# A first mixer's output projection with eight products instead of seven, and three moved steps

## The chip, the cores and the metric

The kernel runs on one core of a Trainium2 chip. The metric is the time of one execution on the device in microseconds (us), as the median of several runs. PE is TensorE (matmuls), PEld its weight loads, DVE VectorE, ACT ScalarE, POOL GpSimd, and SP the engine whose queue issues most of the DMAs.

## The reference, cut to what matters

A trunk of two layers on 512 tokens of width 1024. Each layer is a mixer, a cross-attention into 256 memory rows (4 heads of 256), and a gated MLP with a width-3 convolution; each sub-layer ends in `x = layer_norm(alpha * x + f(x))`. The first layer's mixer, which most of the change touches:

```python
proj = x @ w_in                                   # 1024 -> 1536
uv = gelu(proj[..., :1024]); u, v = uv[..., :512], uv[..., 512:]
v = layer_norm(v, ln_g, ln_b)
sp = einsum('gij,bnjgc->bnigc', masked(w_s), v in blocks of 128) + b_s
y_a = u * sp                                      # "gates", 4 groups of 128 channels
xb = proj[..., 1024:]                             # 4 groups, trailing means of 2, 4, 8, 16 tokens
pooled = trailing_mean(xb, window) - xb
y_b = einsum('bsgc,gcd->bsgd', pooled, pool_w) * pool_scale
return concatenate([y_a, y_b]) @ w_out            # 1024 -> 1024
```

The second layer's mixer is `w_out(B * conv3(C * h))` with `B, C, h` from one projection. All is float32.

## The kernel before, in words

**Precision.** Every operand of a matmul is split in two parts: `split` casts it on ACT to a high part (L86) and subtracts that on DVE for a low part (L87). `mm3` (L226 to L228) adds three matmuls, high x high, high x low and low x high. So each weight tile of 128 x 1024 costs one ACT cast and one DVE subtraction, and so does each activation.

**Weights.** `plan` lists all weight tiles in the order of use. `Weights.load` fetches up to three ahead by DMA into one of 7 `raw` tiles and splits the next into one of RING = 5 buffer pairs (`wh`, `wl`); each `weights.done()` sets off one such load when a tile has been used.

**Plain and fast products.** A plain output projection (`residual_norm`, L513 to L544) works by halves of 512 output columns. The first half runs over the 8 blocks of k, with the 4 token blocks t inside, into 4 PSUM banks, and then adds each bank to `xt[t]` (L491). The second half holds all four weight tiles, does one token block at a time, adds it, takes statistics (L499) and normalises it (`norm`, L336 to L341); at k = 2 of token blocks 2 and 3 it transposes blocks 0 and 1 of the new x (`to_feat`, L366). The transposes of blocks 2 and 3 are returned as a hook for the next stage.

A fast product (`fast_product`) does 7 block products in place of 8, in the manner of Strassen and Winograd. It needs sums of blocks on both sides: for the activations `Blocks` keeps two neighbouring feature blocks of y in a scratch tile and makes S1 to S4 of them on DVE (L277), then splits three or four blocks at a time (`act<-blocks`); for the weights POOL makes the sums t1 to t4 (L162, L169 to L171) from the raw tiles. It adds 16 banks to x (L382) where the plain form adds 8. `norm(3)` and both pairs of transposes are returned as hooks. Fast forms serve the first mixer's `ab_w_out`, the second's `c_w_out`, and the MLP's down projections but for the last group of layer 1.

**The first mixer** (`mixer_ab`): the v projection over tokens, its layer norm, four feature blocks of `ab_w_f` with the trailing means, then four feature blocks for u, each with its gelu (L615); pool blocks (`pool_block`) and gate blocks (`gate_block`) are woven in between them, and the y blocks go into `Blocks`. `FIRST` turns the order of the weights by two, since the pool halves come first.

**What follows.** `proj_k` makes the keys of layer 0's attention with 256-column matmuls, 24 to a weight tile; the hooks run ahead of its heads 1, 2 and 3. In layer 1, `proj_v` does, after the mixer's product. `attend` then does queries, scores with the softmax (DVE maximum, ACT exponential), `turn(h)` (transposes of head h's softmax) and `values(h)`.

**The order on each engine** is laid at build time by a planner, which takes the instructions that its own model holds ready, earlier ones in the program first; the hardware then runs each engine's list in that order. PSUM has 8 banks, all from one pool; activations share 12 slots.

Of the kernel before, what the change touches and what calls it, by code (L numbers as in the profile page):

```python
# [8 lines left out]
F32 = mybir.dt.float32  # L9
# [21 lines left out]
AHEAD = 3  # L31
FFN_GROUPS = (((0, 8), (8, 14), (14, 22)), ((0, 8), (8, 16), (16, 22)))
PAD = 16
FIRST = {"ab_w_out": 2}


@with_exitstack
def kernel(ctx: ExitStack, tc: tile.TileContext, a: dict, out: bass.AP):
# [73 lines left out]
    plan = []  # L112
    for layer in range(2):
        if layer == 0:
            plan += [("ab_w_v", i) for i in range(4)] + [("ab_w_f", i) for i in range(4)] + [("pool_w",)]
            plan += [("ab_w_f", i) for i in range(4, 8)]
            plan += fast_plan("ab_w_out", 0, 0, 4)
            plan += [("xa_wk", layer, i) for i in range(8)]
        else:
            plan += [("xa_wk", layer, i) for i in range(8)]  # L120
            plan += [("c_w_in", i) for i in range(24)]
            plan += fast_plan("c_w_out", 0, 0, 4)
        wq = [("xa_wq", layer, i) for i in range(8)]
        wv = [("xa_wv", layer, n, i) for n in range(2) for i in range(4)]
        plan += wv + wq if layer else wq + wv
        plan += [("xa_wo", layer, n, i) for n in range(2) for i in range(4)]
        for m0, m1 in FFN_GROUPS[layer]:
            plan += [("ffn_w_up", layer, i) for i in range(2 * m0, 2 * m1)]
            if layer == 0 or m1 < NF:
                plan += fast_plan("ffn_w_down", layer, m0 // 2, m1 // 2)  # L130
            else:
                plan += [("ffn_w_down", layer, n, i) for n in range(2) for i in range(m0 // 2, m1 // 2)]

    class Weights:
# [7 lines left out]
        def fast(self, what, name, layer, i, i0=None, i1=None):  # L142

            w = a[name][layer]
            half = [slice(0, 512), slice(512, CH)]

            def fetch(src):
                t = raw_tile()
                nc.sync.dma_start(t[:, : src.shape[-1]], src)
                return t  # L150

            def both(key, make=raw_tile):
                if key not in self.kept:
                    self.kept[key] = make()
                    self.sides[key] = 0
                self.sides[key] += 1
                return self.kept[key][:, half[self.sides[key] - 1]]

            at = (i + FIRST.get(name, 0)) % w.shape[1]
            if what == "b11b21":  # L160
                w0, w1 = fetch(w[0, at]), fetch(w[1, at][:, half[0]])
                nc.gpsimd.tensor_sub(both("t1"), w1[:, half[0]], w0[:, half[0]])  # L162
                return w0
            if what == "t2b22":
                w1, w0 = fetch(w[1, at]), fetch(w[0, at])
                self.turn += i == i0
                t3 = both(("t3", i0), lambda: row_tile("gb"[self.turn % 2]))
                b12 = t2 = w1[:, half[0]]
                nc.gpsimd.tensor_sub(t3, w1[:, half[1]], b12)  # L169
                nc.gpsimd.tensor_add(t2, t3, w0[:, half[0]])  # L170
                nc.gpsimd.tensor_sub(both(("t4", i0)), w0[:, half[1]], t2)  # L171
                return w1
            t = self.kept.pop({"t1t1": "t1", "t4t4": ("t4", i), "t3t3": ("t3", i)}[what])
            return t[:, : 512 * (i0 - i)]
# [372 lines left out]


    def mixer_ab(xT):
        vs, pads = slot(F32), slot(F32)  # L550
        v = [vs[:, t * 512 : (t + 1) * 512] for t in range(NT)]
        ps = [ps_tile() for _ in range(NT)]
        for k in range(KD):
            if k % 2 == 0:
                w = weights.take("ab_w_v", k // 2)
            for t in range(NT):
                proj_tok(ps[t], xT, k, t, w, k % 2, k == 0, k == KD - 1)
            if k % 2:
                weights.done()
        g, b = load_rows("sgu_ln_g", 0, AW, nc.sync), load_rows("sgu_ln_b", 0, AW, nc.sync)  # L560
        for t in range(NT):
            nc.scalar.activation(v[t], ps[t], AF.Gelu_apprx_tanh)
            st = spool.tile([P, 1, 6], F32, tag="stats1", name=nm("st"))
            nc.vector.bn_stats(st[:, 0, :], v[t])
            normalise(v[t], st, g, b)

        pooled = Act(4)
        for gi, win in enumerate(WINDOWS):
            (ps,) = proj_batch([("ab_w_f", gi)], xT)
            cur, *free = [pads[:, j * (PAD + S) : (j + 1) * (PAD + S)] for j in range(3)]  # L570
            xb = cur
            nc.gpsimd.memset(cur[:, :PAD], 0.0)
            nc.scalar.copy(cur[:, PAD:], ps)
            sh, lo = 1, 0
            while sh < win:
                nxt = free[0]
                lo += sh
                nc.vector.tensor_add(nxt[:, lo:], cur[:, lo:], cur[:, lo - sh : PAD + S - sh])
                free = [cur if cur is not xb else free[1]]
                cur, sh = nxt, sh * 2  # L580
            pl = tmp()
            e = win - 1
            nc.vector.scalar_tensor_tensor(pl, cur[:, PAD:], 1.0 / win, xb[:, PAD:], op0=ALU.mult, op1=ALU.subtract)
            nc.vector.tensor_mul(pl[:, :e], cur[:, PAD : PAD + e], inv[:, :e])
            nc.vector.tensor_sub(pl[:, :e], pl[:, :e], xb[:, PAD : PAD + e])
            split(pooled.h(gi), pooled.l(gi), pl)


        wsT, bsb = load_consts()
        y, pw = Blocks(), weights.take("pool_w")  # L590

        def pool_block(gi):
            ps = ps_tile()
            c = slice(gi * P, (gi + 1) * P)
            mm3(ps, pw[0][:, c], pw[1][:, c], pooled.h(gi), pooled.l(gi), True, True)
            y.put(gi, lambda to: nc.scalar.activation(to, ps.rearrange("p (i s) -> p i s", i=2), AF.Copy, scale=pscale[:, gi : gi + 1]))

        def gate_block(gi, ut):
            ps = ps_tile()
            for t in range(NT):  # L600
                nc.tensor.matmul(ps[:, t * P : (t + 1) * P], v[t][:, gi * P : (gi + 1) * P], wsT[:, gi, :], start=True, stop=True)
            sp = tmp()
            nc.vector.tensor_tensor(
                sp.rearrange("p (n i) -> p n i", n=NT),
                ps.rearrange("p (n i) -> p n i", n=NT),
                bsb[:, gi : gi + 1, :].to_broadcast([P, NT, P]),
                op=ALU.add,
            )
            y.put(gi, lambda to: nc.vector.tensor_mul(to, *(t.rearrange("p (i s) -> p i s", i=2) for t in (sp, ut))))

        last = None
        for gi in range(4):
            (ps,) = proj_batch([("ab_w_f", 4 + gi)], xT)
            ut = tmp()
            nc.scalar.activation(ut, ps, AF.Gelu_apprx_tanh)  # L615
            if gi < 2:
                pool_block(2 * gi)
                pool_block(2 * gi + 1)
            if gi == 1:
                weights.done()  # L620
            if last:
                gate_block(*last)
            last = gi, ut
        gate_block(*last)
        return y

    def conv3(dst, src, tap, bias=None):
# [62 lines left out]
    def attend(layer, xT, kT, v):  # L690
# [55 lines left out]
        if v is None:  # L746
            for m in range(8):
                queries(m, m + 1)
            o, v, mem = Act(8), {}, load_mem()
            scores(0)  # L750
            v[0] = proj_v(layer, mem, 0)
            turn(0)
            scores(1)
            values(0)
            v[1] = proj_v(layer, mem, 1)
            turn(1)
            scores(2)
            values(1)
        else:
            for m in range(6):  # L760
                queries(m, m + 1)
            scores(0)
            queries(6, 7)
            scores(1)
            queries(7, 8)
            o = Act(8)
            turn(0)
            scores(2)
            values(0)
            turn(1)  # L770
            values(1)

        def second():
# [45 lines left out]
    for layer in range(2):  # L819
        if layer == 0:  # L820
            y = mixer_ab(xT)
            xT, left = residual_norm([(lambda: y, 0, 8)], "ab_w_out", "ln_mix", layer, ahead=load_ahead)
            kT = proj_k(layer, mem.pop(), dict(zip((1, 2, 3), left)))
            v = None
        else:
            kT = proj_k(layer, mem.pop(), dict(zip((1, 2, 3), left)))
            y = mixer_c(xT)
            xT, left = residual_norm([(lambda: y, 0, 8)], "c_w_out", "ln_mix", layer, ahead=load_ahead)
            v = {0: proj_v(layer, mem[0], 0, {4: left[0]}), 1: proj_v(layer, mem.pop(), 1, {0: left[1], 6: left[2]})}
        o, hooks = attend(layer, xT, kT, v)  # L830
        xT, left = residual_norm([(lambda: o, 0, 8)], "xa_wo", "ln_xa", layer, hooks=hooks)
        up = [(lambda m0=m0, m1=m1, xT=xT, late=left[0]: ffn_up(layer, xT, late, m0, m1), m0, m1) for m0, m1 in FFN_GROUPS[layer]]
# [76 lines left out]
```

## Time and profile before

| | us |
|---|---|
| median of 3 runs | 1351.86 |
| lowest, highest | 1350.41, 1353.79 |
| the profiled execution | 1348.82 |
| its span, first to last instruction | 1347.1 |

| engine | busy us | share of the span |
|---|---|---|
| PE | 1320.3 | 98% |
| PEld (beside PE) | 1108.6 | 82% |
| DVE | 912.7 | 68% |
| ACT | 519.8 | 39% |
| POOL | 220.5 | 16% |

The share is a mean over stages with different limits. PE's idle time is put down, in the profile, to the instruction that ended it: `<-DVE x L382` is a wait until DVE had done line 382. The granted clock is PE's, 1.00 being full speed; matmuls are pipelined, so the time from one start to the next is what one costs, not the duration in its row. A name such as `ps<-act,wh` reads: bank from moving operand, stationary operand.

### The profile page before, as it was taken

How to read it: one execution, taken by the hardware profiler on the slowest of the kernel's cores; microseconds unless marked ns; L12 is line 12 of the kernel's file. 1: busy time of each engine (PE TensorE's matmuls, PEld its weight loads, DVE VectorE, ACT ScalarE, POOL GpSimd, SP SyncE). 2: the span in 40 equal slices, each digit the busy share in tenths (PEclk: the TensorE clock that was granted, in tenths of full speed). 3: DMA queues.
4: the chain of work that ended last, by engine and by line, in shares of the span. 5: the costliest groups of instructions: out<-in, count | busy, mean ns of one | idle time of the engine just before them, and what ended most of it. 6: DMA issues, size and time to landing. Idle time of an engine off the chain costs nothing. (4 is left out here: it accounts for less than half of the span.)

```text
span 1347.1 us, 16309 instructions
## 1 busy us (share of the span) xinstructions
PE 1320.3 (98%) x6373; PEld 1108.6 (82%) x6373; DVE 912.7 (68%) x1165; ACT 519.8 (39%) x665; POOL 220.5 (16%) x176
## 2 busy tenths in 40 slices
PE   9988999999999999999999999999999999999997
PEld 7867988889888888887988887788898888888885
DVE  6898746586676676669945569846676685577446
ACT  6444435324443443434423334434144343343330
POOL 1251100010240220033100142100000330141001
PEclk9989999999999999999999999999999999999999
DMA  8536634122345244236433237531133353236301
GB/s 315 164 111 203 203 109 149 54 80 86 102 146 159 82 138 156 86 118 224 157 110 104 81 108 249 189 94 47 47 94 102 111 179 118 86 115 229 94 0 63
DMA packets 50621, 170.51 MB, mean 127 GB/s; under 512 B 6000, under 2 KB 6128, under 8 KB 50544
## 3 DMA queue, kind: packets, MB, share of 16 engines
q1 hardware_dynamic: 48816, 163.18, 37.3%
q0 software_dynamic: 1728, 6.29, 1.5%
q8 instruction: 50, 0.82, 0.2%
q14 instruction: 27, 0.22, 0.0%
HBM read 167.35 MB, written 2.10 MB: 126 GB/s over the span
## 5 line engine op out<-in xcount | busy, mean ns | idle before, releaser
L87 DVE TENSOR_TENSOR wl<-raw,wh 128x1024 fp32r<-128x1024 f32 (+1 forms) x279 | 351.0, 1265 | 241.4 <-ACT wh L86 238.2
L86 ACT CAST wh<-raw 128x1024 fp32r<-128x1024 f32 (+1 forms) x279 | 290.7, 1042 | 518.1 <-PE ps L227 283.3
L226 PE MATMUL ps<-act,wh 128*128 128x512 f32 (+1 forms) x1284 | 472.5, 369 | 1.2 <-DVE act L87 1.1
L227 PE MATMUL ps<-act,wh 128*128 128x512 f32 (+1 forms) x1284 | 472.5, 368 | 0.1
L228 PE MATMUL ps<-act,wl 128*128 128x512 f32 (+1 forms) x1284 | 472.4, 368 | 0.0
L226 PEld LDWEIGHTS ps<-act,wh 128*128 128x128 f32 x1284 | 241.9, 189 | 42.2 <-DVE act L87 2.3
L227 PEld LDWEIGHTS ps<-act,wh 128*128 128x128 f32 x1284 | 242.1, 189 | 40.4 <-DVE act L87 0.4
L228 PEld LDWEIGHTS ps<-act,wl 128*128 128x128 f32 x1284 | 242.0, 189 | 40.1
L226 PE MATMUL ps<-wh,act 128*128 128x512 f32 (+1 forms) x656 | 257.1, 393 | 8.4 <-ACT tmp L615 4.6
L227 PE MATMUL ps<-wl,act 128*128 128x512 f32 (+1 forms) x656 | 256.3, 391 | 3.0 <-DVE wl L87 3.0
L228 PE MATMUL ps<-wh,act 128*128 128x512 f32 (+1 forms) x656 | 255.5, 389 | 0.0
L226 PEld LDWEIGHTS ps<-wh,act 128*128 128x128 f32 x656 | 124.1, 189 | 37.4 <-DVE x L382 5.9
L227 PEld LDWEIGHTS ps<-wl,act 128*128 128x128 f32 x656 | 124.2, 189 | 30.3 <-DVE wl L87 5.8
L228 PEld LDWEIGHTS ps<-wh,act 128*128 128x128 f32 x656 | 123.9, 189 | 25.3
L338 POOL TENSOR_TENSOR rs<-rs,mhalf 128x1 f32<-128x1 f32 x28 | 39.7, 1418 | 484.0 <-DVE rs L337 484.0
L162 POOL TENSOR_TENSOR raw<-raw,raw 128x512 f32<-128x512 f32 x27 | 39.4, 1460 | 458.9 <-DVE wl L87 379.5
L87 DVE TENSOR_TENSOR act<-blocks,act 128x768 fp32r<-128x768 f32 (+1 forms) x54 | 75.5, 1410 | 9.7 <-ACT act L86 9.7
L86 ACT CAST act<-ps 128x512 fp32r<-128x512 f32 x104 | 56.1, 594 | 60.5 <-PE ps L366 39.3
L382 DVE SCALAR_TENSOR_TENSOR x<-x,ps 128x512 f32<-128x512 f32 x112 | 72.0, 680 | 10.8 <-PE ps L228 10.8
L87 DVE TENSOR_TENSOR act<-ps,act 128x512 fp32r<-128x512 f32 x104 | 67.2, 683 | 12.9 <-ACT act L86 12.9
L86 ACT CAST act<-blocks 128x768 fp32r<-128x768 f32 (+1 forms) x54 | 49.1, 942 | 64.6 <-DVE blocks L277 64.6
L793 DVE TENSOR_TENSOR blocks<-tmp,ps 128x512 f32<-128x512 f32 x38 | 26.1, 688 | 59.8 <-PE ps L228 58.4
(80 smaller groups left out, 859.2 us busy)
## 6 DMA issues: line engine op xcount, KB each, us to landing
raw<-in_ffn_w_up SPq DMA_DIRECT2D x88, 512.0 KB, 3.6
raw<-in_ffn_w_down SPq DMA_DIRECT2D x63, 512.0 KB, 3.6
raw<-in_c_w_in SPq DMA_DIRECT2D x24, 512.0 KB, 3.5
raw<-in_xa_wk SPq DMA_DIRECT2D x16, 512.0 KB, 4.8
raw<-in_xa_wq SPq DMA_DIRECT2D x16, 512.0 KB, 3.6
raw<-in_xa_wv SPq DMA_DIRECT2D x16, 512.0 KB, 4.7
raw<-in_xa_wo SPq DMA_DIRECT2D x16, 512.0 KB, 4.0
raw<-in_ab_w_out SPq DMA_DIRECT2D x12, 512.0 KB, 3.6
```

Of the source, the lines that this page charges most:

```text
L86: nc.scalar.copy(h, src)
L87: nc.vector.tensor_sub(l, src, h.bitcast(F32))
L162: nc.gpsimd.tensor_sub(both("t1"), w1[:, half[0]], w0[:, half[0]])
L226: nc.tensor.matmul(ps, lh, rh, start=start, stop=False, skip_group_check=more)
L227: nc.tensor.matmul(ps, lh, rl, start=False, stop=False, skip_group_check=more)
L228: nc.tensor.matmul(ps, ll, rh, start=False, stop=stop, skip_group_check=more)
L338: nc.gpsimd.tensor_tensor(rs, rs, mhalf, op=ALU.pow)
L382: return nc.vector.scalar_tensor_tensor(z, z, scale, ps, op0=ALU.mult, op1=ALU.add)
L793: hid.put(m, lambda to: nc.vector.tensor_mul(to, *(v.rearrange("p (i s) -> p i s", i=2) for v in (g, ps[2 * i + 1]))))
```

## The change

1. **The first mixer in the plain form.** The four u blocks come first, and their gelus go into a slot of their own; then four gate blocks, then four pool blocks, each split into an ordinary activation (`Act`). `pool_w` moves behind the u weights in the plan.
2. **Its output projection in the plain form:** eight weight tiles in place of fourteen, no block sums, norms and the transposes of token blocks 0 and 1 within the product. Only the transposes of blocks 2 and 3 remain as a hook, at `proj_k`'s head 2. The `FIRST` turn goes.
3. **Layer 1:** `norm(3)` behind the fast `c_w_out` moves from k = 4 to k = 2 of the first `proj_v`, and the transposes of blocks 2 and 3 from k = 6 to k = 5 of the second.
4. **Layer 1's attention:** `turn(1)` stands ahead of `values(0)`.

```diff
-            plan += [("ab_w_v", i) for i in range(4)] + [("ab_w_f", i) for i in range(4)] + [("pool_w",)]
-            plan += [("ab_w_f", i) for i in range(4, 8)]
-            plan += fast_plan("ab_w_out", 0, 0, 4)
+            plan += [("ab_w_v", i) for i in range(4)] + [("ab_w_f", i) for i in range(8)] + [("pool_w",)]
+            plan += [("ab_w_out", 0, n, i) for n in range(2) for i in range(4)]
...
-        vs, pads = slot(F32), slot(F32)
+        vs, us, pads = slot(F32), slot(F32), slot(F32)
...
         wsT, bsb = load_consts()
-        y, pw = Blocks(), weights.take("pool_w")
...
+        u = []
+        for gi in range(4):
+            (ps,) = proj_batch([("ab_w_f", 4 + gi)], xT)
+            ut = us[:, gi * 512 : (gi + 1) * 512]
+            nc.scalar.activation(ut, ps, AF.Gelu_apprx_tanh)
+            u.append(ut)
+
+        y = Act(8)
+        pw = weights.take("pool_w")
+        for gi in range(4):
             ps = ps_tile()
             for t in range(NT):
                 nc.tensor.matmul(ps[:, t * P : (t + 1) * P], v[t][:, gi * P : (gi + 1) * P], wsT[:, gi, :], start=True, stop=True)
...
-            y.put(gi, lambda to: nc.vector.tensor_mul(to, *(t.rearrange("p (i s) -> p i s", i=2) for t in (sp, ut))))
+            nc.vector.tensor_mul(sp, sp, u[gi])
+            split(y.h(gi), y.l(gi), sp)
         for gi in range(4):
+            ps = ps_tile()
+            c = slice(gi * P, (gi + 1) * P)
+            mm3(ps, pw[0][:, c], pw[1][:, c], pooled.h(gi), pooled.l(gi), True, True)
+            yb = tmp()
+            nc.scalar.activation(yb, ps, AF.Copy, scale=pscale[:, gi : gi + 1])
+            split(y.h(4 + gi), y.l(4 + gi), yb)
+        weights.done()
         return y
...
             o = Act(8)
             turn(0)
             scores(2)
+            turn(1)
             values(0)
-            turn(1)
             values(1)
...
-            kT = proj_k(layer, mem.pop(), dict(zip((1, 2, 3), left)))
+            kT = proj_k(layer, mem.pop(), {2: left[0]})
...
-            v = {0: proj_v(layer, mem[0], 0, {4: left[0]}), 1: proj_v(layer, mem.pop(), 1, {0: left[1], 6: left[2]})}
+            v = {0: proj_v(layer, mem[0], 0, {2: left[0]}), 1: proj_v(layer, mem.pop(), 1, {0: left[1], 5: left[2]})}
```

More of the change, by code (lines that the diff above doesn't have):

```diff
@@ L33 @@
 PAD = 16
-FIRST = {"ab_w_out": 2}
 @with_exitstack
@@ L157, in both @@
                 return self.kept[key][:, half[self.sides[key] - 1]]
-            at = (i + FIRST.get(name, 0)) % w.shape[1]
             if what == "b11b21":
-                w0, w1 = fetch(w[0, at]), fetch(w[1, at][:, half[0]])
+                w0, w1 = fetch(w[0, i]), fetch(w[1, i][:, half[0]])
                 nc.gpsimd.tensor_sub(both("t1"), w1[:, half[0]], w0[:, half[0]])
@@ L164, in fast @@
             if what == "t2b22":
-                w1, w0 = fetch(w[1, at]), fetch(w[0, at])
+                w1, w0 = fetch(w[1, i]), fetch(w[0, i])
                 self.turn += i == i0
@@ L589, in mixer_ab @@
         wsT, bsb = load_consts()
-        y, pw = Blocks(), weights.take("pool_w")
[L592 to L598, printed above, removed]
+        u = []
[7 more added lines that the diff above has]
+        for gi in range(4):
             ps = ps_tile()
@@ L608, in gate_block @@
             )
-            y.put(gi, lambda to: nc.vector.tensor_mul(to, *(t.rearrange("p (i s) -> p i s", i=2) for t in (sp, ut))))
-        last = None
+            nc.vector.tensor_mul(sp, sp, u[gi])
+            split(y.h(gi), y.l(gi), sp)
         for gi in range(4):
[L613 to L624, printed above, removed]
+            ps = ps_tile()
[5 more added lines that the diff above has]
+        weights.done()
         return y
```

## The prediction

> **What bounds the kernel now.** I read the page first (part 1), then busy time by windows, then TensorE (PE) in order of time, then the groups.
>
> ```profile
> PE 1320.3 (98%) x6373; PEld 1108.6 (82%) x6373; DVE 912.7 (68%) x1165; ACT 519.8 (39%) x665; POOL 220.5 (16%) x176
> ```
>
> PE is busy for 98% of the span, so a microsecond counts only if PE stands still or has more or fewer matmuls. The windows say where it stands still. Columns: stretch, length, busy time and instructions of PE, PEld, DVE, ACT, POOL, granted clock, DMA share, GB/s.
>
> ```profile
> 26.84:62.20 35.36, 35.36 (x157) 29.29 (x156) 31.84 (x54) 12.27 (x19) 10.88 (x12) 1.00 0.52 174
> 62.20:76.60 14.40, 14.40 (x82) 12.50 (x80) 12.61 (x15) 8.77 (x11) 6.28 (x5) 1.00 0.39 114
> 76.60:128.64 52.04, 43.32 (x171) 33.73 (x170) 47.73 (x56) 20.16 (x21) 18.62 (x12) 0.90 0.55 175
> 128.64:156.39 27.75, 27.00 (x225) 26.49 (x224) 27.75 (x39) 13.74 (x19) 4.95 (x5) 1.00 0.57 185
> ```
>
> The first row is projections without a pause: six feature blocks of 24 matmuls and four pool blocks of 3, 156 in 35.36 us, so one 512-column matmul costs **0.2267 us** of PE. The third row is the first output projection, from its first matmul to the first one of proj_k. Its seven half-products are 7 x 4 pairs x 2 halves x 3 = 168 matmuls, 38.08 us at that pace; it took 52.04. **13.96 us are lost there**. In order of time (start, duration, and in brackets the idle time with what ended it):
>
> ```profile
> 80.13 0.40 PE L228 MATMUL ps<-wh,act 128*128 128x512 f32 x1
> 85.16 0.80 PE L226 MATMUL ps<-wh,act 128*128 128x512 f32 x1 [4.63 <-ACT tmp L615]
> 89.55 0.40 PE L227 MATMUL ps<-wl,act 128*128 128x512 f32 x1
> ...
> 102.71 0.50 PE L226 MATMUL ps<-wh,act 128*128 128x512 f32 x1 [1.20 <-DVE x L382]
> ...
> 113.07 0.39 PE L226 MATMUL ps<-wh,act 128*128 128x512 f32 x1
> 115.40 0.50 PE L227 MATMUL ps<-wl,act 128*128 128x512 f32 x1 [1.95 <-DVE wl L87]
> 117.13 0.80 PE L226 MATMUL ps<-wh,act 128*128 128x512 f32 x1 [0.77 <-DVE x L382]
> 120.25 0.39 PE L227 MATMUL ps<-wl,act 128*128 128x512 f32 x1
> ```
>
> From 80.13 to 89.55 eleven matmuls start: 9.42 - 11 x 0.2267 = 6.93 us lost, of which 4.63 is the wait and 2.30 mostly the lower clock behind it. From 113.07 to 120.25, eleven again: 7.18 - 2.49 = 4.69 lost. Behind the 4.63 stands this on ACT:
>
> ```profile
> 81.89 1.78 ACT L86 CAST act<-blocks 128x768 fp32r<-128x768 f32 x2 [6.21 <-DVE blocks L277]
> 83.58 1.04 ACT L86 CAST wh<-raw 128x1024 fp32r<-128x1024 f32 x1
> 84.52 0.59 ACT L615 ACTIVATE tmp<-ps 128x512 f32<-128x512 f32 x1
> ```
>
> The last gelu (L615) had its bank full before the product began, but stood behind casts of block sums that DVE had not made; the product wanted that bank. All four waits of the stretch lead to DVE, which is busy 47.73 of 52.04 us. So here the chip is bound by DVE, not by PE.
>
> **The change part by part.** *The plain product.* It has 2 halves x 8 k x 4 t x 3 = 192 matmuls, 24 more: **+5.44 us** of PE, on the path. What it takes off DVE, by groups of 26.84 to 160 us (mean ns after the comma):
>
> ```profile
> L87 DVE TENSOR_TENSOR wl<-raw,wh 128x1024 fp32r<-128x1024 f32 (+1 forms) x30 | 41.1, 1384 | 4.5 <-ACT wh L86 4.4
> L87 DVE TENSOR_TENSOR act<-blocks,act 128x768 fp32r<-128x768 f32 (+1 forms) x8 | 10.8, 1372 | 2.1 <-ACT act L86 2.1
> L382 DVE SCALAR_TENSOR_TENSOR x<-x,ps 128x512 f32<-128x512 f32 x16 | 10.3, 677 | 0.0
> L277 DVE TENSOR_TENSOR blocks<-blocks 128x256 f32<-128x256 f32 x16 | 7.5, 481 | 0.3
> L609 DVE TENSOR_TENSOR blocks<-tmp,tmp 128x512 f32<-128x512 f32 x4 | 3.7, 954 | 0.0
> L87 DVE TENSOR_TENSOR act<-tmp,act 128x512 fp32r<-128x512 f32 x4 | 2.8, 690 | 2.1 <-ACT act L86 2.1
> ```
>
> Weight splits go from 14 to 8 (6 x 1.384 = 8.3 us), the 16 block sums go (7.5), eight block splits (10.8) become eight of 0.690 (5.5), and 16 adds to x become 8 (5.4 saved): 8.3 + 7.5 + 10.8 - 5.5 + 5.4 = 26.5 us less DVE work. That is nearly twice the 13.96 us lost, so I take the loss as gone: **-13.96 us**. The 16 weight sums on POOL and eight of the 16 weight loads in SP's queue go too; neither was on the path. The two row loads in POOL's queue move ahead of the product, into a queue with nothing else.
>
> Is the plain form free of waits? The kernel has it next door, the layer's xa_wo; second half and what follows it:
>
> ```profile
> 267.20:293.20 26.00, 26.00 (x124) 21.64 (x123) 21.97 (x32) 6.26 (x8) 4.37 (x3) 1.00 0.15 49
> 293.20:302.00 8.80, 8.80 (x76) 8.80 (x75) 7.52 (x10) 1.06 (x1) 1.46 (x1) 1.00 0.64 216
> ...
> 294.03 1.22 DVE L87 TENSOR_TENSOR wl<-raw,wh 128x1024 fp32r<-128x1024 f32 x1
> 295.77 1.21 DVE L87 TENSOR_TENSOR wl<-raw,wh 128x1024 fp32r<-128x1024 f32 x1
> 297.01 1.17 DVE L87 TENSOR_TENSOR wl<-raw,wh 128x1024 fp32r<-128x1024 f32 x1
> ```
>
> PE is busy throughout. The second half holds four of the five weight buffers to its end, so four loads must be split around the handover; three of these are ready 2.1, 3.8 and 5.0 us after 293.20. The follower there runs 256-column matmuls, 24 to a weight, as proj_k does, so it asks as fast as proj_k will. Adding load_mem's two splits (1.2 us each by the nearest wl rows) at the head of that half is hidden by the 4 us that DVE is idle in 26. Exit: 0.
>
> *The entry.* After: eight feature blocks from 26.84 end at 26.84 + 8 x 5.44 = 70.4; gates take 14.40 - 2 x 5.44 = 3.5, pools 2.7, so the product still starts at about 76.6. The first y: 71.2 + an add from a bank (0.677, as L382's) + L609's 0.954 + a cast (0.6, as L615's 0.59) + a split of 0.690 = 74.2, in time. Later gates follow DVE at 2.32 us each, and the k loop eats one in 12 x 0.2267 = 2.72. Banks bind more: eight are taken by gates and pools, and the fourth token block needs the fourth gate's add, at 71.2 + 3 x 2.32 + 0.68 = 78.9, where PE wants it at 76.6 + 3 x 0.68 = 78.6. **+0.3 us**. Ends: 0, and 2.7, which is the 1.20 of L382 (a bank that waits for an add) with a slow clock behind it: 117.13 to 120.25 holds 7 matmuls and loses 1.53. I take the near end since DVE's share of block work in 62.20:76.60 leaves. Moving pool_w behind the u weights only brings those sooner.
>
> [...]
>
> *Transposes beside proj_k.* Sixteen of 32 move into the product at the same PE cost. This wait was on a bank that DVE, full in 128.64:156.39, freed late:
>
> ```profile
> 149.43 1.16 PE L366 MATMUL ps<-ident,x 128*128 128x128 f32 x8 [0.75 <-DVE act L87]
> ```
>
> ```profile
> 301.75 1.91 PE L366 MATMUL ps<-ident,x 128*128 128x128 f32 x16
> ```
>
> After xa_wo (second row) the same sixteen run without it. **-0.75** (ends -0.75 and 0). norm(3) leaves proj_k's hooks for the product, where 301.75 shows it in time.
>
> *Layer 1's transposes.* norm(3) comes two k blocks sooner, to_feat(2,3) one.
>
> ```profile
> 828.17:859.00 30.83, 29.46 (x137) 23.99 (x136) 30.71 (x42) 12.59 (x14) 7.12 (x6) 1.00 0.62 201
> ```
>
> ```profile
> 868.09 1.10 PE L226 MATMUL ps<-act,wh 128*128 128x512 f32 x2 [1.12 <-DVE act L87]
> ```
>
> The first query waits 1.12 us for the split of those transposes. DVE is full here (30.71 of 30.83) and gets no less work, so order alone decides: best -1.12; worst +0.6, had norm(3) pushed a weight split back. I take **0**.
>
> *Head 1's transposes ahead of head 0's values.*
>
> ```profile
> 924.38 1.03 PE L733 MATMUL ps<-ident,tmp 128*128 128x128 f32 x8
> 926.66 0.73 PE L226 MATMUL ps<-act,act 128*128 128x512 f32 x2 [1.24 <-ACT act L86]
> ```
>
> ```profile
> 923.22 0.59 ACT L86 CAST act<-ps 128x512 fp32r<-128x512 f32 x1 [2.82 <-PE ps L228]
> 923.70 0.48 ACT L721 ACTIVATE tmp<-ps,mx 128x256 f32<-128x256 f32 x1
> ```
>
> values(1) waits 1.24 us for a cast that stands behind head 2's exponentials, which begin at 923.70. The transposes would come 12 x 0.2267 = 2.7 us sooner, 921.7 to 922.5, while ACT idles 2.82 us before 923.22. **-1.2** (ends -1.24, and 0 if the exponentials stay ahead).
>
> **Sum:** -13.96 + 5.44 + 0.3 - 0.75 + 0 - 1.2 = **-10.2 us**. The profiled execution (1348.82 us, 3.04 below the median of the runs, 1351.86) would take 1338.6; on the median, **1341.7**. Bounds: -13.96 + 5.44 - 0.75 - 1.12 - 1.24 = -11.6 (1340.2), and -13.96 + 5.44 + 2.7 + 0.6 = -5.2 (1346.7).
>
> **The rivals.** *An engine queue blocks at the entry, as now.* ACT takes casts of y in order, and a gelu or pool copy behind one that waits for DVE holds a bank again: the 6.93 us of 80.13 to 89.55 instead of 0.3. For it: that row is in this very place. Against: each y waits for one product on DVE, not for four block sums. -10.2 + 6.6 = -3.6: 1348.3.
>
> *Refills late at the exit.* proj_k wants its second weight after 24 matmuls of 8.80 / 76 = 0.116 us, 2.8 us. If the planner puts the last token block's sums and norm ahead of all four splits, that weight comes as late as the last refill does behind xa_wo, 5.0 us: 2.2 us of waiting and 1.53 of slow clock. For it: the loads stand last in the program. Against: behind xa_wo the first is there at 2.1. -10.2 + 3.7 = -6.5: 1345.4.
>
> *Slower: the first y comes as late as the last gate blocks do now.* The plain loop reads gate 0 first and cannot start on anything else; the block form starts on pool blocks, ready early. If DVE's order puts the gates behind all else, y(0) is split when the last gate blocks are now:
>
> ```profile
> 93.28 3.19 DVE L87 TENSOR_TENSOR act<-blocks,act 128x768 fp32r<-128x768 f32 x2
> ```
>
> 93.28 - 76.60 = 16.7 us of waiting: -10.2 - 0.3 + 16.7 = +6.2, 1358.1. Slower by 0.3% from a wait of 14.6 us up. Against: what delayed that row, three pairs of block sums and splits, is gone.
>
> **How the numbers follow.** A change below 0.3% (4.1 us) can't be told from none. The likeliest case 0.62 (1341.7; own range 1340.2 to 1346.7); late refills 0.10, faster still; a blocked queue 0.15, within 0.3%; a late first y 0.13, slower. Faster 0.72, same 0.15, slower 0.13. The range runs from 1339.0 (the best bound less about 1 us of the runs' own spread, 1350.41 to 1353.79) to 1349.0 (past the blocked queue), and leaves out the late y.
>
> **What would show it.** 192 matmuls from about 76.6 to about 122, with 16 transposes among them; DVE well under full from 76 to 150; no wait for L615; no L366 wait in layer 0's proj_k; values(1) without the 1.24; the query's 1.12 about as now. PE idle over 10 us between 70 and 100, or four weight waits behind the product, would make the forecast wrong.

## The result, and the profile after

The changed kernel takes **1339.68 us** (median of four runs, 1337.86 to 1340.83) against 1351.13 for the kernel before on the same chip (four runs, 1349.1 to 1353.79): a ratio of 0.9913, 95% interval 0.989 to 0.9935. It is faster by 11.45 us by the medians. The profiled execution took 1340.83 us, with a span of 1339.1.

First the page's busy times, as in the prediction's first fence:

```profile
PE 1322.8 (99%) x6397; PEld 1113.0 (83%) x6397; DVE 880.7 (66%) x1135; ACT 511.2 (38%) x659; POOL 190.3 (14%) x160
```

PE has 24 instructions more, as counted ahead, and its busy time grew by 2.5 us. That growth isn't in the stretch of the change: there, in the windows below, PE is busy 70.08 us after 70.32, since the 24 matmuls more (5.44 us) are paid by matmuls that no longer run at a slow clock (0.94 before, 1.00 now). It lies in places that the change leaves alone, one of which is shown near the end. DVE lost 32.0 us (912.7 to 880.7) and POOL 30.2.

Then the windows of the kernel after, from the first matmul of the output projection to the first of `proj_k`, from there to the first query of layer 0, and both together; and, for that last stretch, the kernel before. Columns as in the prediction.

```profile
77.51:122.83 45.32, 45.32 (x210) 37.70 (x208) 34.64 (x48) 17.71 (x24) 4.50 (x3) 1.00 0.28 86
122.83:147.59 24.76, 24.76 (x209) 24.76 (x208) 20.04 (x24) 11.79 (x15) 2.58 (x3) 1.00 0.72 248
77.51:147.59 70.08, 70.08 (x417) 62.47 (x416) 54.68 (x71) 29.50 (x39) 7.08 (x6) 1.00 0.44 143
```

```profile
76.60:156.39 79.79, 70.32 (x395) 60.22 (x394) 75.48 (x94) 33.90 (x40) 23.57 (x16) 0.94 0.56 178
```

PE is busy through all 70.08 us, at a clock of 1.00, and DVE has fallen from 75.48 busy of 79.79 to 54.68 of 70.08. The stretch is 9.71 us shorter; the prediction's terms for it (-13.96, +5.44, +0.3, -0.75) give -8.97.

The two other waits that the change aimed at, in the kernel after: the first query of layer 1, and the casts of head 1's transposes.

```profile
861.40 0.49 PE L223 MATMUL ps<-act,wh 128*128 128x512 f32 x1 [0.28 <-DVE act L86]
862.09 0.47 PE L223 MATMUL ps<-act,wh 128*128 128x512 f32 x1 [0.20 <-DVE act L86]
...
915.53 1.08 ACT L85 CAST act<-ps 128x512 fp32r<-128x512 f32 x2 [1.86 <-PE ps L724]
916.63 0.48 ACT L712 ACTIVATE tmp<-ps,mx 128x256 f32<-128x256 f32 x1
```

The query's 1.12 has become 0.28 + 0.20. The casts (915.53) now stand ahead of head 2's exponentials (916.63), and the values have no wait any more.

### The profile page after: what moved, and what is told of

Its sections match the earlier page's. It is cut to its first block, busy times and chain, and to the rows that moved or that the text cites. A ratio compares the mean times of both kernels' runs of the same rounds, so it can differ in the third digit from the quotient of the medians.

```text
span 1339.1 us, 16258 instructions
## 1 busy us (share of the span) xinstructions
PE 1322.8 (99%) x6397; PEld 1113.0 (83%) x6397; DVE 880.7 (66%) x1135; ACT 511.2 (38%) x659; POOL 190.3 (14%) x160
## 4 chain that ended last, share of the span: by engine, by line
PE 92%; DVE 5%; issue 1%; DMA 1%; ACT 0%; POOL 0%; POOLq 0%; DVEq 0%; ACTq 0%
PE ps L223 30%; PE ps L224 30%; PE ps L225 30%; DVE wl L86 2%; PE ps L363 1%; DVE act L86 1%; DMA raw<-in_memT 1%; DVE x L338 1%; PE ps L724 1%; DVE stats L496 0%; DVE x L379 0%; POOL rs L335 0%; PE ps L798 0%; DVE x L336 0%; PE ps L598 0%
## 5 line engine op out<-in xcount | busy, mean ns | idle before, releaser
L86 DVE TENSOR_TENSOR wl<-raw,wh 128x1024 fp32r<-128x1024 f32 (+1 forms) x275 | 344.6, 1259 | 267.0 <-ACT wh L85 259.7
L85 ACT CAST wh<-raw 128x1024 fp32r<-128x1024 f32 (+1 forms) x275 | 286.5, 1042 | 540.1 <-PE ps L224 310.5
L223 PEld LDWEIGHTS ps<-wh,act 128*128 128x128 f32 x664 | 125.6, 189 | 28.8 <-DVE x L379 3.1
L225 PEld LDWEIGHTS ps<-wh,act 128*128 128x128 f32 x664 | 125.2, 189 | 25.6
L159 POOL TENSOR_TENSOR raw<-raw,raw 128x512 f32<-128x512 f32 x23 | 32.6, 1415 | 449.7 <-DVE wl L86 375.1
L379 DVE SCALAR_TENSOR_TENSOR x<-x,ps 128x512 f32<-128x512 f32 x96 | 61.6, 679 | 9.8 <-PE ps L225 9.8
L86 DVE TENSOR_TENSOR act<-blocks,act 128x768 fp32r<-128x768 f32 (+1 forms) x46 | 61.5, 1349 | 8.5 <-ACT act L85 8.5
L625 DVE SCALAR_TENSOR_TENSOR tmp<-ps,convw,tmp 128x511 f32<-128x511 f32 x88 | 65.6, 745 | 1.6
```

The costliest lines, as they stand in the source:

```text
L85: nc.scalar.copy(h, src)
L86: nc.vector.tensor_sub(l, src, h.bitcast(F32))
L223: nc.tensor.matmul(ps, lh, rh, start=start, stop=False, skip_group_check=more)
L225: nc.tensor.matmul(ps, ll, rh, start=False, stop=stop, skip_group_check=more)
L379: return nc.vector.scalar_tensor_tensor(z, z, scale, ps, op0=ALU.mult, op1=ALU.add)
L625: nc.vector.scalar_tensor_tensor(dst[:, s:], src[:, : S - s], tap(2 - s), dst[:, s:], op0=ALU.mult, op1=ALU.add)
```

## The experiments

The question was where the 13.96 us of the old product came from, since that decides what the plain form was worth. Theories: DVE has too much work of its own (the prediction's); the order in ACT's queue (a gelu behind casts); POOL's weight sums, by coming late or by slowing DVE beside them (the prediction had put these sums off the path). "Product" below is the time from its first matmul to the first of `proj_k`; "stretch" runs on to the first query. Before: product 52.04, stretch 79.79. After: 45.32 and 70.08. Two of the runs below, part 4 alone and part 3 alone, leave the old product as it was, and their profiles show how far one profile's stretch can be trusted:

```profile
77.45:156.66 79.21, 68.40 (x395) 58.58 (x394) 75.51 (x93) 33.91 (x40) 23.01 (x16) 0.98 0.56 182
76.99:154.91 77.92, 68.98 (x396) 59.64 (x394) 75.32 (x93) 34.02 (x40) 21.53 (x16) 0.96 0.55 183
```

The same code took 77.92 to 79.79 us, so a difference below 2 us against the old stretch says nothing. By these three profiles the plain form is worth 7.8 to 9.7 us of the stretch.

### The parts of the change alone

Parts 1 and 2 alone, with layer 1 left as it was:

```diff
-    y, pw = Blocks(), weights.take("pool_w")
+    y = Act(8)      # u blocks, gates, pools; plain ab_w_out, as in the change
-    kT = proj_k(layer, mem.pop(), dict(zip((1, 2, 3), left)))
+    kT = proj_k(layer, mem.pop(), {2: left[0]})
```

> The kernel before with the plain mixer, its plain product and the one hook in proj_k; layer 1 is left as it was. Theory: the gain comes from DVE's backlog around the first product, so nearly all of it is here. From the product's first matmul to the first query 70.1 us as after the change (79.8 before), time 8 to 10 us under the kernel before. Rival: layer 1's edits carry a good part; then this kernel gains 6 us or less.

Measured: 1339.95 us against 1350.27, ratio 0.9929 (0.9911 to 0.9946).

```profile
77.15:147.22 70.07, 70.07 (x417) 62.46 (x416) 54.66 (x71) 29.56 (x39) 7.09 (x6) 1.00 0.44 143
```

The stretch is that of the full change, so nearly all the gain stands here. Layer 1 keeps its waits of 1.12 and 1.23.

Part 4 alone:

```diff
+            turn(1)
             values(0)
-            turn(1)
             values(1)
```

> The kernel before with turn(1) ahead of values(0) alone. Theory: values(1) loses its wait of 1.24 us for an ACT cast, and the restart behind it: 1.2 to 1.6 us less between head 0's transposes and the next product, 0.1% of the time, so no difference that rounds can show; the trace must show the wait gone. Rival: the exponentials stay ahead of the cast on ACT, and the same wait comes back at the same place: 0.

Measured: 1349.03, ratio 1.0 (0.9987 to 1.0012). In the trace the wait of 1.24 is gone; the time can't tell a gain of 1.2 from none.

Part 3 alone:

```diff
-0, {4: left[0]}), 1: proj_v(layer, mem.pop(), 1, {0: left[1], 6: left[2]})
+0, {2: left[0]}), 1: proj_v(layer, mem.pop(), 1, {0: left[1], 5: left[2]})
```

> The kernel before with norm(3) two blocks and the last transposes one block sooner in layer 1's proj_v alone. Theory: DVE is full there and its work is the same, but the transposes' splits come ahead of weight splits, so the first query's wait falls from 1.12 to about 0.5 us (as after the change), 0.9 us in all. Rival: order alone decides nothing, and the wait stays at 1.1. A third possibility: it costs, where norm(3) pushes a weight split back: a wait of PE for wl inside proj_v, up to 0.6.

Measured: 1347.53, ratio 0.9987 (0.9975 to 0.9999).

```profile
865.92 0.50 PE L226 MATMUL ps<-act,wh 128*128 128x512 f32 x1 [0.28 <-DVE act L87]
866.61 0.47 PE L226 MATMUL ps<-act,wh 128*128 128x512 f32 x1 [0.19 <-DVE act L87]
```

1.12 became 0.47: the step that I had put at 0 is worth some 0.65 us. Which of its two hooks does it was asked of the kernel after, with `norm(3)` put back at k = 4:

```diff
-0, {2: left[0]}), 1: proj_v(layer, mem.pop(), 1, {0: left[1], 5: left[2]})
+0, {4: left[0]}), 1: proj_v(layer, mem.pop(), 1, {0: left[1], 5: left[2]})
```

> The kernel after with layer 1's norm(3) back at k = 4 (to_feat(2,3) stays one block sooner). It tells which of the two moved hooks shortened the first query's wait of layer 1 from 1.12 to 0.28 + 0.20 us. If the transposes' place did: wait about 0.5 as in after. If norm(3)'s place did: 1.1 again, time about 0.8 us above after's 1339.7, which is near what the rounds can tell.

Measured: 1337.82 against 1350.97, ratio 0.9901 (0.9885 to 0.9916). Its first query waits only 0.19, and for a weight's cast. So the transposes' earlier place shortens the wait, and `norm(3)`'s does nothing for it. This is the lowest ratio of the kernels that leave no work out, but its interval overlaps that of the change (0.989 to 0.9935): no better version is shown.

### The order of the mixer

The fast product kept, with the mixer in the new order, so that no gelu stands behind casts of block sums:

```diff
-        last = None
+        u = []          # four u blocks and their gelus, then pool_w
...
+        for gi in range(4): pool_block(gi)
+        for gi in range(4): gate_block(gi, u[gi])
```

> The kernel before with the fast product kept, but all four u blocks and their gelus ahead of the pool and gate blocks, so that no gelu can stand behind a cast of block sums. DVE's work is the same. Theory (DVE's backlog): the 4.63 us wait for the gelu goes, but waits for DVE take its place at the product's entry; from the product's first matmul to the first query 77 us or more (79.8 before), time within 3 us of the kernel before. Rival (ACT's queue order alone): the 6.93 us of that wait with its slow clock are gained, 72.9 us for the stretch, time 7 us under the kernel before.

Measured: **1354.52, ratio 1.0041 (1.0026 to 1.0056)**, slower, by more than the 3 us that the theory allowed. Windows of the product and of the stretch, and the longest waits:

```profile
77.94:135.88 57.94, 44.85 (x170) 34.62 (x169) 51.96 (x66) 23.07 (x24) 14.88 (x10) 0.88 0.47 153
77.94:162.67 84.73, 71.64 (x393) 61.13 (x393) 78.51 (x101) 36.81 (x43) 18.99 (x14) 0.92 0.51 166
```

```profile
96.73 0.79 PE L225 MATMUL ps<-wh,act 128*128 128x512 f32 x1 [6.40 <-ACT act L86]
107.31 0.80 PE L225 MATMUL ps<-wh,act 128*128 128x512 f32 x1 [3.63 <-ACT act L86]
```

The wait for the gelu is gone, and PE now stands before the casts of the block sums themselves, for longer: a stretch of 84.73, where the rival asked for 72.9. The old 4.63 at L615 was where the lateness showed, not its cause: the order in ACT's queue falls. The reverse, the plain product behind the old woven mixer:

```diff
+        y, pw = Act(8), weights.take("pool_w")   # pools and gates woven into the u blocks
```

> The plain product behind the mixer as it was: pool and gate blocks woven between the u blocks, each split as an ordinary activation. Theory: without block sums DVE has room for either order, so the stretch from the product's first matmul to the first query is 70 to 71 us as after the change, time within 0.1% of the plain mixer's. Rival: the order of the mixer is part of the gain; then 2 us or more are lost at the product's entry.

Measured: 1343.87 against 1353.04, ratio 0.9925 (0.9901 to 0.9949).

```profile
76.92:147.09 70.17, 70.17 (x419) 62.54 (x418) 52.16 (x67) 24.34 (x30) 8.23 (x6) 1.00 0.44 143
```

70.17 without a wait. The plain product brings the gain in either order; the first mixer's new order brings nothing of its own that these runs can show.

### Taking work off the fast product

The sums S1 to S4 on DVE left out (POOL sets those blocks to zero; what the product computes is no longer the output projection):

```diff
-                    nc.vector.tensor_tensor(f[:, to, :], f[:, x, :], f[:, y, :], op=op)
+                    nc.gpsimd.memset(f[:, to, :], 0.0)
```

> The kernel before without DVE's sums of the first mixer's blocks: S1 to S4 are zeros, set by POOL; all splits and matmuls stay. Theory: 16 x 0.481 = 7.5 us of DVE work go, and as DVE is the bound there the stretch from the product's first matmul to the first query falls by 5 to 8 us, to 72 to 75. Rival (the weights' side is what is late): a fall of 2 us or less.

Measured: 1343.9, ratio 0.9937 (0.9916 to 0.9957). Product, then stretch:

```profile
76.93:120.49 43.56, 40.98 (x171) 32.52 (x170) 40.44 (x45) 19.65 (x20) 16.25 (x16) 0.96 0.64 209
76.93:148.78 71.85, 67.98 (x395) 59.02 (x394) 68.29 (x83) 33.43 (x39) 22.35 (x20) 0.98 0.62 200
```

7.5 us less DVE work by the prediction's row shortened the product by 52.04 - 43.56 = 8.48 us and the stretch by 7.94, or by 6.1 against the shortest of the three old stretches. So DVE does bound this product, and a microsecond of its work is worth about one there. Part of the saving is clock: in the product PE stands still for 2.58 us instead of 8.72, and its busy time too is 2.34 shorter, at a granted clock of 0.96 instead of 0.90. Of the loss, 43.56 - 38.08 = 5.48 us are left.

Now POOL's weight sums left out, with DVE's own list untouched (three of the four sums are constants, so the output is another one):

```diff
-                nc.gpsimd.tensor_sub(both("t1"), w1[:, half[0]], w0[:, half[0]])
+                nc.gpsimd.memset(both("t1"), 0.0)      # and t3, t4; t2 is left as loaded
```

> The kernel before without POOL's sums of the first product's weights: t1, t3 and t4 are zeros and t2 is taken unsummed; all splits, matmuls and loads stay. Theory (DVE's backlog): POOL's sums cost through DVE, whose operations in 26.84 to 160 us last longer beside them (weight splits 1.38 us on average against 1.22 alone, block splits 1.37 against about 1.1, and others); some 8 us of DVE time go, and the stretch from the product's first matmul to the first query falls from 79.8 to 72 to 75 us. Rival: POOL is beside the path, and the stretch stays at 78 to 80.

Measured, with two runs: **1337.67 against 1353.04, ratio 0.9886 (0.9859 to 0.9914)**.

```profile
76.76:114.97 38.21, 38.21 (x172) 31.62 (x170) 35.63 (x47) 17.79 (x19) 3.64 (x5) 1.00 0.66 211
76.76:143.25 66.49, 65.21 (x396) 58.12 (x395) 63.47 (x85) 31.54 (x38) 9.71 (x9) 1.00 0.61 199
```

168 matmuls at 0.2267 are 38.08: of 13.96 us lost, 0.13 are left. I had set these sums aside, and without them nothing of the loss remains; the stretch of 66.49 lies below what either theory gave. (All 16 loads stay in this run, so the eight that the change drops were not what cost.) The sums are not the whole cause by themselves, since more than half of the loss also goes without DVE's block sums: read together, the two runs say that DVE has just enough time for its own work here, and that POOL's sums take that margin away. Either they came late, or they slowed DVE. DVE's groups from 26 to 160 us, first the kernel before, then the run without the sums:

```profile
L87 DVE TENSOR_TENSOR wl<-raw,wh 128x1024 fp32r<-128x1024 f32 x29 | 40.4, 1408 | 4.5 <-ACT wh L86 4.4
```

```profile
L87 DVE TENSOR_TENSOR wl<-raw,wh 128x1024 fp32r<-128x1024 f32 x31 | 37.4, 1221 | 8.0 <-ACT wh L86 7.8
L284 DVE TENSOR_TENSOR blocks<-blocks 128x256 f32<-128x256 f32 x16 | 6.6, 422 | 0.3
L616 DVE TENSOR_TENSOR blocks<-tmp,tmp 128x512 f32<-128x512 f32 x4 | 2.7, 688 | 0.0
```

The same weight split costs 1.408 us on the mean in the kernel with the sums and 1.221 without. In order of time, in the kernel before, DVE and then POOL:

```profile
66.22 2.31 DVE L87 TENSOR_TENSOR wl<-raw,wh 128x1024 fp32r<-128x1024 f32 x1
...
70.66 1.22 DVE L87 TENSOR_TENSOR wl<-raw,wh 128x1024 fp32r<-128x1024 f32 x1
...
76.59 2.32 DVE L87 TENSOR_TENSOR wl<-raw,wh 128x1024 fp32r<-128x1024 f32 x1
78.83 0.68 DVE L603 TENSOR_TENSOR tmp<-ps,act 128x512 f32<-128x512 f32 x1
```

```profile
65.58 1.87 POOL L170 TENSOR_TENSOR raw<-row,raw 128x512 f32<-128x512 f32 x1 [1.23 <-DMA raw<-in_ab_w_out]
68.67 1.34 POOL L171 TENSOR_TENSOR raw<-raw,raw 128x512 f32<-128x512 f32 x1 [1.23 <-DVE wl L87]
...
76.13 1.70 POOL L170 TENSOR_TENSOR raw<-row,raw 128x512 f32<-128x512 f32 x1 [1.26 <-DMA raw<-in_ab_w_out]
77.90 2.16 POOL L171 TENSOR_TENSOR raw<-raw,raw 128x512 f32<-128x512 f32 x1
```

The split that begins while POOL's 65.58 runs takes 2.31, the one at 70.66, when POOL stands still, 1.22, and the one behind 76.13 again 2.32. The add at 78.83, which reads one operand from a bank, keeps its 0.68 beside POOL's 77.90. DVE's "busy" time thus held standing time.

To tell the neighbour from the lateness, the run without sums got 16 POOL subtractions whose results nobody reads:

```diff
+                    for t in (t3, t4, t4):
+                        nc.gpsimd.tensor_sub(scratch, t, t)   # and one on t1
```

> The kernel before with the weight sums set to constants as in the run without them (so the first mixer's output is another one), and then 16 subtractions on POOL of 128x512, at the places of the sums, that read those constants and write a scratch tile which nothing reads. No load, no split and no matmul waits for them. Theory 'neighbour' (a POOL operation beside DVE's two-input operations makes these longer, whatever POOL works on): the splits wl<-raw,wh between 60 and 130 us take 1.35 us or more again on the mean (1.20 without the sums), and most of the 13.3 us between 66.49 and 79.79 comes back: first matmul of the product to first query 74 to 79 us, time about 1345 to 1350. Theory 'lateness' (the sums cost time because the matmuls' weights and the buffers wait for them): nothing comes back, 66 to 68 us, time about 1338.

Measured: **1350.76 against 1350.97, ratio 0.9998 (0.9985 to 1.0011)**: the whole gain is gone again.

```profile
77.09:126.76 49.67, 42.20 (x172) 33.08 (x170) 46.36 (x57) 21.68 (x23) 11.85 (x11) 0.93 0.55 183
77.09:155.04 77.95, 69.19 (x396) 59.57 (x394) 74.20 (x95) 35.43 (x42) 17.92 (x15) 0.96 0.55 184
```

```profile
L87 DVE TENSOR_TENSOR wl<-raw,wh 128x1024 fp32r<-128x1024 f32 x29 | 36.6, 1275 | 3.4 <-ACT wh L86 3.3
L290 DVE TENSOR_TENSOR blocks<-blocks 128x256 f32<-128x256 f32 x16 | 10.1, 639 | 0.3
L622 DVE TENSOR_TENSOR blocks<-tmp,tmp 128x512 f32<-128x512 f32 x4 | 4.3, 1085 | 0.0
```

The stretch is 77.95, inside the 74 to 79 of the neighbour theory, among the three old stretches, and far from 66 to 68. One number of it just missed: between 60 and 130 us the weight splits take 1.332 us on the mean (1.275 in the longer window above), not 1.35 or more. Other operations bear the rest: the block sums, 422 to 639 ns each, which touch no weight, and the gates' products, 688 to 1085. By the rows above these three groups alone cost DVE 3.5 + 1.6 + 1.6 = 6.7 us more. The busy time of the product's window (46.36 where it was 35.63) is no measure of it, since that window holds 57 DVE operations and not 47: it shows the backlog along with the slowing. DVE waited for weight casts 3.3 us in all of 26 to 160, less than without the sums (7.8). What this run can't exclude is a small part of lateness: a `raw` tile that a dummy reads is free for its next load only behind it.

### How much cover the plain form has

The kernel after, with each low part of `ab_w_out` subtracted three times (8 x 2 x 1.22 = 19.5 us more DVE work):

```diff
                 split(h, l, raw)
+                if plan[len_done[0]][0] == "ab_w_out":
+                    for _ in range(2):
+                        nc.vector.tensor_sub(l, raw, h.bitcast(F32))
```

> The changed kernel with the low part of each of the eight ab_w_out weights subtracted three times instead of once: 16 x 1.22 = 19.5 us more work on DVE between about 55 and 102 us, no other change. Theory (DVE is what the fast form lacked): most of it fits into DVE's idle time (10.7 us idle in the product's 45.3, more ahead of it), but two of these weights stand in DVE's list around the gates, so each y is 2.4 to 4.9 us late and the entry wait that was priced at 0.3 and measured at 0 comes to 1 to 4 us, clock included: stretch 71 to 75 us (70.1 after the change). Rival (DVE's load does not matter here): 70.1.

Measured, with two runs (1339.37 and 1343.79): 1341.58 against 1353.04, ratio 0.9915 (0.9882 to 0.9949).

```profile
77.03:148.38 71.35, 70.77 (x417) 62.22 (x416) 65.51 (x83) 30.27 (x40) 8.23 (x6) 1.00 0.45 148
```

The stretch grew by 1.27 us, with two waits of 0.18 and 0.39. So the plain form could bear 19.5 us more on DVE almost for nothing. DVE is busy there for 65.51 of 71.35 us, 92%, and in the old stretch it was for 75.48 of 79.79, 95%: a DVE nearly as full, with no weight sums beside it, hardly holds PE up.

### What is left: the first group of the down projections

Both kernels have the waits there that the old product had. In the kernel after:

```profile
622.65 0.50 PE L224 MATMUL ps<-wl,act 128*128 128x512 f32 x1 [1.21 <-DVE wl L86]
...
624.38 0.58 PE L223 MATMUL ps<-wh,act 128*128 128x512 f32 x1 [0.77 <-DVE x L379]
```

Two tries at them. The first calls `load_mem` earlier in the group:

```diff
+                if norm and j == 2:
+                    norm[2]()
...
-            if norm and i == 0:
-                norm[2]()
```

> The kernel after with one edit: in the down-projections' first group load_mem is called two blocks of matmuls into the half-products rather than at the head of the t2 and b22 loop. In after, four waits stand there: 1.21 on a weight split and 0.77 on an add at 622 to 625 us, 1.01 and 0.77 at 823 to 825. Theory 'order' (the two splits of mem stand ahead of the weight split that the product waits for): these waits go, with some clock behind them, 4 to 7 us over both layers, time 1333 to 1336. Theory 'amount' (DVE has as much to do as it can in this group, wherever mem's splits stand): the waits move to another weight or add, the time stays within 1337 to 1342.

Measured: 1340.21, ratio 0.9913 (0.9898 to 0.9928): no gain. DVE, then PE:

```profile
610.06 2.72 DVE L86 TENSOR_TENSOR act<-raw,act 128x1024 fp32r<-128x1024 f32 x2 [2.02 <-ACT act L85]
```

```profile
613.43 0.50 PE L223 MATMUL ps<-wh,act 128*128 128x512 f32 x1 [2.27 <-DVE x L379]
```

The four waits went, and a new one came, 2.27 here and 2.29 in layer 1: DVE stands 2.02 us for mem's cast, and the adds that free the banks stand behind it. The numbers are those of 'amount', but its cause is not shown: by these rows mem comes too late for the new place in DVE's list, and the group's adds pay. Whether a place in between would do better wasn't tried.

The second puts mem's low parts on POOL:

```diff
-        return [load_split(a["memT"][i], "act") for i in range(2)]
+            nc.scalar.copy(h, raw)
+            nc.gpsimd.tensor_sub(l, raw, h.bitcast(F32))
```

> The kernel after with mem's two low parts subtracted on POOL rather than on DVE, in both layers: 2.4 us less on DVE in each down-projection group, 2 more operations of 128x1024 on POOL each. Theory 'amount of DVE' (that group is short of DVE time): the waits of 622 to 625 and 823 to 825 us shrink, 2 to 4 us less, time 1336 to 1338. Theory 'neighbour' (a POOL operation costs DVE beside it as much as it takes off): the group's DVE operations get longer by as much, time 1339 to 1342 with the waits about as now.

Measured: 1341.52, ratio 0.9923 (0.9905 to 0.9941): no gain. POOL, then DVE:

```profile
610.63 5.77 POOL L646 TENSOR_TENSOR act<-raw,act 128x1024 fp32r<-128x1024 f32 x2
```

```profile
612.33 1.81 DVE L86 TENSOR_TENSOR wl<-raw,wh 128x1024 fp32r<-128x1024 f32 x1 [2.39 <-ACT wh L85]
614.06 3.42 DVE L86 TENSOR_TENSOR wl<-row,wh 128x1024 fp32r<-128x1024 f32 x1
```

A split of 1.22 took 3.42 while POOL held its 5.77. The move took 2.4 us off DVE and cost (1.81 - 1.22) + (3.42 - 1.22) = 2.8 on these two splits alone: the neighbour again, in another place. PE's waits in the group grew with it, to 2.31 and 0.54 us on adds in layer 0 and one of 2.71 in layer 1.

## Why the prediction was right, and where it was not

1341.7 was forecast and 1339.68 measured: inside the stated range (1339.0 to 1349.0), but 0.5 us below the likeliest case's own (1340.2 to 1346.7). Step by step:

- **The plain product.** The 168 matmuls' loss is gone and the 24 more cost their 5.44: 192 x 0.2267 = 43.5 us, and the 16 transposes fill the rest of 45.32. Product and followers run without a wait, as the list of what would show it asked. The 13.96 was read from one profile; the other two of the old product have a stretch that is 0.58 and 1.87 us shorter.
- **The step that failed** is the sentence that POOL's weight sums were not on the path. I read the waits, which all led to DVE, and took DVE's durations as its own work. Without the sums, the old product loses 0.13 us. The sum came out because the change removes them too, along with the DVE work that I counted, and that is partly luck: whether 26.5 us less DVE work would have been enough with POOL's sums still beside it was not run. My 26.5 us is 32.0 on the page. A good part of the difference lies in operations that stay and were longer beside the sums, such as the gates' four products: 954 ns each in the prediction's row of L609, 0.69 us in the kernel after.
- **The entry**, +0.3: no wait there. (Its far end of 2.7 put the slow clock of another place behind the wait of 1.20; the last section has the rows.) The first y was split earlier than PE wanted it; DVE in the kernel after:

```profile
73.40 1.28 DVE L600 TENSOR_TENSOR tmp<-ps,act 128x512 f32<-128x512 f32 x2
74.60 1.28 DVE L606 TENSOR_TENSOR tmp<-tmp,act 128x512 f32<-128x512 f32 x2
...
76.40 1.28 DVE L86 TENSOR_TENSOR act<-tmp,act 128x512 fp32r<-128x512 f32 x2
```

  The planner took the gates in pairs, and the first of two splits begins at 76.40 where the product starts at 77.51. The late first y, the blocked queue and the late refills did not come.
- **Beside `proj_k`**, -0.75: the wait is gone. From `proj_k`'s first matmul to the query the time fell from 27.75 to 24.76, 2.99 less, of which the 16 transposes that moved are 1.7 to 1.8. That leaves some 1.2, so the term was too small by about 0.5.
- **Layer 1's transposes**, 0: measured about -0.65, of the -1.12 at best.
- **Head 1's transposes**, -1.2: the 1.24 is gone, by the mechanism named.

Together -9.71 - 0.65 - 1.24 = -11.6 where -10.2 was forecast, and the medians say -11.45. That is closer than it can be held to: with the shortest old stretch the same sum is -9.7. The two profiles differ by 8.0 only (1348.82 to 1340.83). Most of the gap to 11.6 is in work that the change doesn't touch: the first mixer's feature blocks start 0.85 us later in the profile of after (27.69 against 26.84), and 2.5 us lie in the first group of layer 0's down projections. That group before, after, and in the run with `norm(3)` late:

```profile
602.38:642.45 40.07, 38.81 (x170) 31.31 (x169) 37.09 (x42) 18.32 (x18) 13.65 (x10) 1.00 0.68 227
```

```profile
593.55:636.11 42.56, 40.58 (x170) 32.45 (x169) 36.05 (x42) 18.20 (x18) 12.29 (x10) 0.96 0.65 215
```

```profile
593.43:633.78 40.35, 38.98 (x170) 31.30 (x168) 36.75 (x42) 18.21 (x18) 13.52 (x10) 1.00 0.67 227
```

The last two have the same code there and differ by 2.2 us: the group sits on the edge of its waits. Such places may be what spreads the runs of this kernel; that was not followed further.

## What to carry to other kernels

When all waits lead to an engine that is full, compare its durations for one and the same operation with each other before taking them as work: here 1.22 and 2.31 us for one split stood in the trace of before, and the times of the long ones pointed at POOL. A saving of TensorE time that is paid for with sums on POOL and DVE is judged by the windows in which these run; here a product with an eighth fewer matmuls lost to the plain one (52.04 us against 43.5 without its transposes), and would have won (38.21) had POOL's sums cost nothing. An engine with low busy time (here POOL, 16%) is not off the path for that.

## What the runs showed of the hardware

A weight split on DVE took longer when it began while POOL worked on whole tiles: 2.31 and 2.32 us beside sums of 128x512, and 3.42 beside the 128x1024 of the last try, against 1.22 with POOL standing still. The add with an operand in a bank, which began beside such a sum too, didn't (0.68). POOL's memsets stretched no split that these traces show: in the run with the dummy subtractions, the split that began at 66.25, while two memsets ran (0.99 together, from 65.51), took 1.22, and in the run without sums, where POOL has memsets in their place, the splits take 1.221 on the mean. Nor did POOL's one-column operations of `normalise`: in the kernel before, DVE's L339 at 123.88 kept its 1.27 beside the POOL row of 1.53 at 124.05, and the weight split that began at 146.27, while the POOL row of 1.52 at 145.24 ran, took 1.22.

The clock did not follow the length of a wait alone. One wait of 2.27 us in layer 0 left the group's clock at 1.00, and the like wait of 2.29 in layer 1 went with 0.97, in the same run (the try with `load_mem` earlier):

```profile
592.86:633.73 40.87, 38.60 (x169) 31.38 (x168) 36.41 (x42) 18.32 (x18) 12.40 (x10) 1.00 0.66 221
792.07:845.29 53.22, 50.93 (x217) 41.47 (x216) 47.56 (x57) 23.14 (x23) 13.72 (x10) 0.97 0.59 197
```

What decided between the two, no run here shows.

The entry's far end of 2.7 us put the loss of 117.13 to 120.25, where most starts are 0.43 apart behind waits of 1.95 and 0.77, behind a wait of 1.20. The wait that it priced, the 1.20 at 102.71 in the kernel before, shows no such pace: the next matmuls start at 103.05 and 103.29, 0.34 and 0.24 us apart, where most starts behind the 4.63 are 0.43 apart. For that wait alone 1.2 was the better end, and no run of the plain product reached 2.7.
